# A two-layer hybrid decoder: sigmoid gates as hyperbolic tangents, and other places for weight blocks, token sums and small steps

## The chip, the cores and the metric

The kernel runs on one core of a Trainium2 chip. The metric is the device time of one execution in microseconds (us), lower is better. The engines are named as in the profile: PE multiplies matrices, PEld loads its stationary side, DVE (VectorE) and ACT (ScalarE) do elementwise work, POOL (GpSimd) does small elementwise work and issues accumulating DMAs, SP issues the other DMAs. Each engine works through its own instructions strictly in order.

## The reference

Two layers over 512 tokens of width 1024, all in float32:

```python
def hybrid_layer(x, ...):
    z = rmsnorm(x, norm_mix) @ w_in          # q_a k_a v_a | q_m k_m v_m o_m if_m | gates
    att = sliding_window_attention(...)      # 8 query heads, 2 key heads, window 128
    hm = rmsnorm(mlstm_chunkwise(...), m_head_norm)
    hm = hm * jax.nn.sigmoid(o_m)
    g_a, g_m = jnp.split(gates, 2, axis=-1)
    mixed = jax.nn.sigmoid(g_a) * (att @ w_att_branch) + jax.nn.sigmoid(g_m) * (hm @ w_m_branch)
    x = x + mixed @ w_out
    u = jax.nn.relu(rmsnorm(x, norm_ffn) @ w_ff1)
    return x + (u * u) @ w_ff2
```

So a layer has three sets of sigmoids: gate A (1024 x 512 values), gate M (as many) and the output gate `o_m` (512 x 512).

## The kernel before, in words

Every float32 matrix is split into a high part (`wh`, `ah`: ACT copies it to the matmul's rounded type) and a low part (`wl`, `al`: DVE subtracts the high part), and a product is three matmuls: high with high, high with low, low with high (`mm3`). So each weight block costs one DMA, one ACT copy and one DVE subtraction before PE can use it. `chunk` does this for the ordinary products: a raw tile `w` (pool `wraw`, 3 of them), then `wh` and `wl` (pool `wsp`, 4 of each), so the splits can run at most some blocks ahead of PE.

A layer has a mixer (function `mixer`) and an MLP. In the mixer, `weave` lays out the program: a row of filling matmul steps with a width of 0.25 each (a unit of 1.0 is one weight block of 12 wide matmuls), and side steps put in at chosen places on that scale. The recording layer then orders the instructions of each engine from it by priority and readiness, so a place is a wish and not an address. The filling row is: mLSTM queries and keys (8 blocks), gates 0 and 1 (gate A, `s0`, `s1`, 8 blocks each), product 2, the attention branch (`a_steps(0)`, `a_steps(1)`, 4 blocks each), products 5, 1, 3, 6, 7, 4 (4 short blocks of 6 wide matmuls each), gates 2 and 3 (gate M, `s2`, `s3`). Products 1 to 7 compute the mLSTM values and output gates with seven half-size products in place of eight: their weights are raw blocks `wa[k]` and `wb[k]` (k = 0 to 3) that are loaded by `begin` and `begin_other` and changed between products by accumulating DMAs on POOL's queue (`more`), and their tokens are sums of quarters of the normed input (`sums1`, `sums_next`, `sums3`, split by `sum_parts`).

The side steps are the attention's pieces (scores, softmax with Exp, transposed probabilities, output; places 7 to 24.2), the mLSTM gating (`gating0` to `gating3`: sums, a running maximum of four scans on DVE in `gating2`, its transposes on PE in `gating3`), the splits of queries and keys (`qk_split`), the mLSTM weights (`m_weights`: Exp) and outputs (`m_out`), and at the end the head norm `m_norm` (its `rsqrt` is Ln and then Exp on ACT) and the transposes of the heads (`head_tr`), which the last products need.

ACT holds one table set at a time. Exp and Ln are used from a set that has both (`LN_EXP`); Sigmoid is in another. The kernel before batches the sigmoids: `gates_a` runs the eight of gate A after the attention, `gates_o` the four output gates after product 4, `gates_m` the eight of gate M after the head norm's Exp, and `back` loads `LN_EXP` again.

Tiles of 128 x 512 come from two pools: `slot()` (pool `act`, 32 tiles) and `temp()` (pool `tmp`, 17 tiles). A tile is handed out again when its last user is done.

Of the kernel before, what the change touches and what calls it, by code (L numbers as in the profile page):

```python
# [33 lines left out]
def hybrid_kernel(ctx, tc, x, norm_mix, w_in, att_q_norm, att_k_norm, att_sinks, m_gate_bias,  # L34
# [199 lines left out]
    last_exp = [None]  # L234

    def rsqrt(dst, v, tag):

        shape = list(v.shape)
        t = sm(shape, tag + "t")
        sc.activation(t, v, AF.Ln)  # L240
        last_exp[0] = sc.activation(dst, t, AF.Exp, scale=-0.5)
# [148 lines left out]
    def mixer(l, norm, late, order, phase):  # L390
# [136 lines left out]
        for i, v_ in enumerate((v4[:, :NB - 1], dv4)):  # L527
            sc.activation(v2[:, i, :, :, 0, :], v_, AF.Copy)
            ve.tensor_tensor(v2[:, i, :, :, 1, :], v_, f32(v2[:, i, :, :, 0, :]), op=ALU.subtract)
# [16 lines left out]
        qT, sps, parts, att_last = {}, {}, {}, [None]  # L546
# [93 lines left out]
        def att_out(b, kv):  # L640
            po = aux()
            ls = parts[b, kv]
            for n, (pr, vb) in enumerate(ls):
                for m, p_ in enumerate(pr):
                    pe.matmul(po, vb.rearrange("p i d -> p (i d)"), p_, start=n + m == 0, stop=n == len(ls) - 1 and m == 1)
            low, both = temp(), temp()
            sc.activation(low[0:64, :], po[64:128, :], AF.Copy)
            p4, l4 = (t[0:64, :].rearrange("p (j i t) -> p j i t", j=2, i=2) for t in (po, low))
            b3 = both[:, 0:2 * P].rearrange("p (j t) -> p j t", j=2)
            for i in range(2):  # L650
                ve.tensor_tensor(b3[64 * i:64 * i + 64], p4[:, :, i, :], l4[:, :, i, :], op=ALU.add)
            for j in range(2):
                dh, dl = (a[:, b * P:(b + 1) * P] for a in att_acts[2 * kv + j])
                att_last[0] = sc.activation(dh, b3[:, j, :], AF.Copy)
                ve.tensor_tensor(dl, b3[:, j, :], f32(dh), op=ALU.subtract)
# [30 lines left out]
        def sigmoid(tiles):  # L686
            for t in tiles:
                i = sc.activation(t, t, AF.Sigmoid)
            return i

        def back(i):

            with tc.issue_after(i.ins):
                sc.preload_act_table_set(LN_EXP)  # L694

        def gate_steps(g, then=lambda: None):
            sg = []

            def ev(m, ps):
                sg.append(slot())  # L700
                ve.tensor_tensor(sg[m], ps, row[0], op=ALU.mult)  # L701
                if m == 3:
                    then()

            return sg, feat_steps(acts, wcols(C_G + 512 * g, 512), ev)
# [22 lines left out]
        def begin(k):  # L728
            wa[k] = temp()
            load(wa[k], 0, 0, k)  # L730
            gp.dma_start(wa[k], block(0, 1, k), accum_op=ALU.add)

        def begin_other(k):
            wb[k] = temp()
# [17 lines left out]
        def sum_parts(key, src):  # L752
            get = ((lambda: slot(F32R, (P, 2, H))) if key in (3, 6)
                   else lambda: now["tmp"].tile([P, 2, H], F32R, tag="t", name=nm("t")))
            sums[key] = [split(src[:, 2 * p:2 * p + 2, :], get=get) for p in range(2)]
# [44 lines left out]
        def gates_o():  # L800
            for b in range(NB):
                last = sc.activation(so[b], so[b], AF.Sigmoid, scale=norm.col[:, b:b + 1])
            back(last)
# [9 lines left out]
        def vo_step(n, k, i):  # L813
# [13 lines left out]
            if k == 3:  # L827
# [3 lines left out]
                if n == 4 and i == 1:  # L831
                    gates_o()
# [8 lines left out]
        for i, (b, kv) in enumerate(units):  # L841
# [6 lines left out]
            if kv == 0 and b + 1 < NB:  # L848
                if b + 2 < NB:
                    side += [(at + 1, lambda b=b: k_vec(b + 2)), (at + 1, lambda b=b: q_vec(b + 2))]  # L850
                side += [(at + 2 * 1.65 - 1.75, lambda b=b: k_tr(b + 1)), (at + 2 * 1.65 - 2.15, lambda b=b: q_tr(b + 1))]
        side += [(8.45, gating0), (25.5, gating1), (28.0, gating2), (30.5, gating3)]
        side += [(at, lambda m=m, i=i: qk_split(m, i))
                 for at, m, i in ((36.0, 0, 0), (36.6, 2, 0), (37.2, 0, 1), (37.8, 2, 1),
                                  (43.0, 1, 0), (43.8, 3, 0), (44.6, 1, 1), (45.4, 3, 1))]
        g0, s0 = gate_steps(0)
        def gates_a():
            with tc.issue_after(att_last[0].ins):
                back(sigmoid(g0 + g1))

        g1, s1 = gate_steps(1)
        side.append((7 + 1.65 * 7 + 3.45 + 2.2 + 0.01, gates_a))
# [30 lines left out]
        def m_out(h, t):  # L893
# [11 lines left out]
            if h:  # L905
                m_gate(h, t)

        def m_gate(h, t):
            c = slice(h * MV, (h + 1) * MV)
            ve.tensor_tensor(hm[t][:, c], hm[t][:, c], so[t][:, c], op=ALU.mult)  # L910
# [11 lines left out]
        def a_steps(g, sg):  # L922
            def ev_a(m, ps):
                t = sg[m]
                prod.append(t)
                ve.tensor_tensor(t, t, ps, op=ALU.mult)  # L926
# [4 lines left out]
        side += [(26.0 + 0.5 * k, lambda k=k: begin(k)) for k in range(4)]  # L931
        side += [(29.0 + 0.5 * k, lambda k=k: begin_other(k)) for k in range(4)]
# [516 lines left out]

    def turn_behind(norm, k):  # L1450

        with tc.issue_after(latest[0].ins):
# [4 lines left out]
            + [(6.5, lambda: gains(grow, 16))]  # L1457
# [53 lines left out]
```

## Time and profile before

| | |
|---|---|
| median of three runs | 1306.27 us (1303.46 to 1309.05) |
| the profiled execution | 1309.28 us, its span 1307.6 us |
| PE busy | 1287.5 us, 98% of the span, 6930 matmuls |
| DVE busy | 1012.1 us, 77% |
| ACT busy | 786.7 us, 60% |
| mean granted PE clock | 0.998 |
| places in the span | layer 0: mixer to about 345 us, MLP to about 650 us; layer 1: the same from there |

How to read it: the page's groups carry the line of the program, `out<-in` the names of tiles, `<-` the engine that ended an idle time. A row of the windows view gives, for a stretch from A to B, the busy time and instruction count of each engine, the granted PE clock, the busy share of the DMA engines and what they moved. A matmul's record is drawn longer (0.39 us for 512 columns) than the distance of two starts (0.23 us), so PE's records overlap.

### The profile page before, as it was taken

Reading aid. Unit: us, or ns where it says so; the run is one execution under the profiler, and the core shown is the slowest. Engines: PE = TensorE matmul, PEld = TensorE weight load, DVE = VectorE, ACT = ScalarE, POOL = GpSimd, SP = SyncE. Lnnn points to the kernel's source line nnn. Section 1 sums busy time; section 2 is a strip of 40 time slices with the busy share of each in tenths; the row PEclk is TensorE's granted clock in tenths of the full one; section 3 lists DMA queues with packets and bytes.
Section 4 is the critical chain, followed back from the end, with each engine's and each line's share of the span. In section 5 each row is a group of like instructions: output and inputs, shape, how many; then the busy total and the mean of one; then the engine's idle time right before and its main releaser. Section 6 shows DMA issues by size and latency. Waiting matters only on the chain. (4 is left out here: it accounts for less than half of the span.)

```text
span 1307.6 us, 19237 instructions
## 1 busy us (share of the span) xinstructions
PE 1287.5 (98%) x6930; PEld 1096.0 (84%) x6930; DVE 1012.1 (77%) x1605; ACT 786.7 (60%) x1375; POOL 224.2 (17%) x313
## 2 busy tenths in 40 slices
PE   9999999999999999999999999999999999999998
PEld 6877778888889999999888777788888899999987
DVE  4688888665677897978957888975737878879797
ACT  5567668543465665656554776884535556665563
POOL 4501141000003121131114011410000030311210
PEclk9999999999999999999999999999999999999999
DMA  5422672273358989898224227622714597988953
GB/s 154 110 74 57 154 147 68 68 241 98 97 145 162 230 191 203 204 203 233 33 69 115 64 62 190 117 73 76 254 58 127 137 206 207 203 208 201 208 147 97
DMA packets 135152, 186.01 MB, mean 142 GB/s; under 512 B 10376, under 2 KB 78832, under 8 KB 135056
## 3 DMA queue, kind: packets, MB, share of 16 engines
q1 hardware_dynamic: 94208, 131.82, 32.7%
q0 software_dynamic: 40128, 52.57, 25.6%
q8 instruction: 54, 0.88, 0.3%
q10 hardware_dynamic: 720, 0.40, 0.1%
q14 instruction: 42, 0.34, 0.1%
HBM read 182.65 MB, written 2.10 MB: 141 GB/s over the span
## 5 line engine op out<-in xcount | busy, mean ns | idle before, releaser
L47 PE MATMUL mm<-i,wh 128*128 128x512 f32 (+1 forms) x1280 | 353.9, 362 | 0.2
L1007 ACT ACTIVATE wh<-raw 128x1024 fp32r<-128x1024 f32 x212 | 223.3, 1056 | 188.1 <-PE mm L47 117.1
L1008 DVE TENSOR_TENSOR wl<-raw,wh 128x1024 fp32r<-128x1024 f32 x212 | 255.7, 1222 | 74.2 <-ACT wh L1007 74.2
L47 PEld LDWEIGHTS mm<-i,wh 128*128 128x128 f32 x1280 | 223.5, 189 | 31.3 <-DVE a L701 1.1
L47 PE MATMUL mm<-i,wl 128*128 128x512 f32 (+1 forms) x640 | 228.9, 359 | 0.0
L166 DVE TENSOR_TENSOR wl<-w,wh 128x512 fp32r<-128x512 f32 (+1 forms) x192 | 129.6, 679 | 101.9 <-ACT wh L165 97.4
L165 ACT ACTIVATE wh<-w 128x512 fp32r<-128x512 f32 (+1 forms) x192 | 116.6, 610 | 110.8 <-PE mm L47 77.5
L47 PE MATMUL mm<-wh,uh 128*128 128x512 f32 x440 | 171.8, 390 | 0.0
L47 PE MATMUL mm<-wl,uh 128*128 128x512 f32 x440 | 171.7, 390 | 0.0
L47 PE MATMUL mm<-wh,ul 128*128 128x512 f32 x440 | 171.2, 389 | 0.0
L1167 POOL DMA_DIRECT2D raw<-in_w_ff_dram x48 | 62.2, 1303 | 542.9 <-DMA raw<-in_w_ff_dram 143.9
L47 PEld LDWEIGHTS mm<-i,wl 128*128 128x128 f32 x640 | 121.0, 189 | 18.2 <-DVE wl L1008 0.6
L47 PE MATMUL mm<-wh,a 128*128 128x512 f32 x320 | 104.0, 398 | 0.7 <-ACT wh L724 0.7
L47 PE MATMUL mm<-wh,i 128*128 128x512 f32 (+1 forms) x352 | 101.4, 361 | 1.2 <-ACT wh L165 0.6
L1053 DVE SCALAR_TENSOR_TENSOR x<-mm,ms,x 128x512 f32<-128x512 f32 x126 | 90.8, 747 | 9.8 <-PE mm L47 9.8
L47 PEld LDWEIGHTS mm<-wh,ul 128*128 128x128 f32 x440 | 82.6, 188 | 17.4
L47 PEld LDWEIGHTS mm<-wh,uh 128*128 128x128 f32 x440 | 82.8, 188 | 16.1
L47 PEld LDWEIGHTS mm<-wl,uh 128*128 128x128 f32 x440 | 82.8, 188 | 15.6
L47 PE MATMUL mm<-a,wh 128*128 128x512 f32 x256 | 80.7, 395 | 2.3 <-DVE a L926 2.0
L47 PEld LDWEIGHTS mm<-wh,a 128*128 128x128 f32 x320 | 60.8, 190 | 14.6 <-ACT wh L724 1.5
L47 PEld LDWEIGHTS mm<-wh,i 128*128 128x128 f32 x352 | 61.9, 188 | 12.7 <-DVE i L179 1.8
L47 PE MATMUL aux<-i,wh 128*128 128x256 f32 x384 | 69.5, 283 | 0.0
(284 smaller groups left out, 2369.8 us busy)
## 6 DMA issues: line engine op xcount, KB each, us to landing
raw<-in_w_ff_dram SPq DMA_DIRECT2D x144, 512.0 KB, 5.1
raw<-in_w_ff_dram POOLq DMA_DIRECT2D x84, 512.0 KB, 7.9
w<-in_w_in_dram SPq DMA_DIRECT2D x112, 256.0 KB, 2.7
t<-in_w_in_dram POOLq DMA_DIRECT2D x32, 256.0 KB, 4.9
w<-in_w_out_dram SPq DMA_DIRECT2D x32, 256.0 KB, 3.2
w<-in_w_att_branch_dram SPq DMA_DIRECT2D x16, 256.0 KB, 3.0
t<-in_w_in_dram SPq DMA_DIRECT2D x16, 256.0 KB, 4.6
w<-in_w_m_branch_dram SPq DMA_DIRECT2D x16, 256.0 KB, 2.6
```

Of the source, the lines that this page charges most:

```text
L47: latest[0] = nc.tensor.matmul(*args, **kw)
L165: sc.activation(wh[:, :off], raw[:, :off], AF.Copy)
L166: ve.tensor_tensor(wl[:, :off], raw[:, :off], f32(wh[:, :off]), op=ALU.subtract)
L1007: sc.activation(hi, src, AF.Copy)
L1008: ve.tensor_tensor(lo, src, f32(hi), op=ALU.subtract)
L1053: ve.scalar_tensor_tensor(xh[:, cc], ps[i][:, cc], ms[j][:, b:b + 1], xh[:, cc], op0=ALU.mult, op1=ALU.add)
L1167: gp.dma_start(to[h], src(h, i, j), accum_op=ALU.add)
```

## The change

Since sigmoid(x) is half of 1 + tanh(x/2), the gates become Tanh on ACT with a scale of 0.5, the multiplications with them become (t + 1) times the other factor in one instruction (TENSOR_TENSOR becomes SCALAR_TENSOR_TENSOR), and the halves go into other factors: the attention's values (`v2`, scale 0.5) and the head norm's gain (0.25, in `late_gains`). The output gates have half the norm's column as their scale (`half`).

Each gate group now runs its four Tanh directly behind its evaluation (`ev`, at m = 3); only the last group loads `LN_EXP` again. Tanh is in a table set with Exp, not with Ln, so the program has four table loads in a layer (before the first Tanh, before the head norm's Ln, before its Exp, and at the end) where it had eight.

The raw blocks `wa`, `wb` are in `slot()` tiles and are begun at 24.5 and 28.0 instead of 26.0 and 29.0; all sums of tokens are in `temp()` tiles. `gating2` and `gating3` move from 28.0 and 30.5 to 30.5 and 35.5, the eight `qk_split` from 36.0 to 45.4 to the wider 37.0 to 48.0, `gates_o` from behind product 4 to 49.1, and the output gate's products of head 1 join those of head 0 at 49.3 and later.

```diff
-            sc.activation(v2[:, i, :, :, 0, :], v_, AF.Copy)
-            ve.tensor_tensor(v2[:, i, :, :, 1, :], v_, f32(v2[:, i, :, :, 0, :]), op=ALU.subtract)
+            sc.activation(v2[:, i, :, :, 0, :], v_, AF.Copy, scale=0.5)
+            ve.scalar_tensor_tensor(v2[:, i, :, :, 1, :], v_, 0.5, f32(v2[:, i, :, :, 0, :]), op0=ALU.mult,
+                                    op1=ALU.subtract)
...
-        def sigmoid(tiles):
-            for t in tiles:
-                i = sc.activation(t, t, AF.Sigmoid)
-            return i
-
-        def back(i):
-
-            with tc.issue_after(i.ins):
-                sc.preload_act_table_set(LN_EXP)
-
-        def gate_steps(g, then=lambda: None):
+        half = sm([P, NB], "half", 1)
+        ve.tensor_scalar(half, norm.col, 0.5, None, op0=ALU.mult)
+
+        def gate_steps(g, last=False):
             sg = []
             def ev(m, ps):
                 sg.append(slot())
                 ve.tensor_tensor(sg[m], ps, row[0], op=ALU.mult)
                 if m == 3:
-                    then()
+                    for t in sg:
+                        i = sc.activation(t, t, AF.Tanh, scale=0.5)
+                    if last:
+                        with tc.issue_after(i.ins):
+                            sc.preload_act_table_set(LN_EXP)
...
-            wa[k] = temp()
+            wa[k] = slot()
...
-            wb[k] = temp()
+            wb[k] = slot()
...
-            get = ((lambda: slot(F32R, (P, 2, H))) if key in (3, 6)
-                   else lambda: now["tmp"].tile([P, 2, H], F32R, tag="t", name=nm("t")))
-            sums[key] = [split(src[:, 2 * p:2 * p + 2, :], get=get) for p in range(2)]
+            sums[key] = [split(src[:, 2 * p:2 * p + 2, :],
+                               get=lambda: now["tmp"].tile([P, 2, H], F32R, tag="t", name=nm("t"))) for p in range(2)]
...
         def gates_o():
             for b in range(NB):
-                last = sc.activation(so[b], so[b], AF.Sigmoid, scale=norm.col[:, b:b + 1])
-            back(last)
+                sc.activation(so[b], so[b], AF.Tanh, scale=half[:, b:b + 1])
...
-                if n == 4 and i == 1:
-                    gates_o()
...
-        side += [(8.45, gating0), (25.5, gating1), (28.0, gating2), (30.5, gating3)]
+        side += [(8.45, gating0), (25.5, gating1), (30.5, gating2), (35.5, gating3)]
...
-                 for at, m, i in ((36.0, 0, 0), (36.6, 2, 0), (37.2, 0, 1), (37.8, 2, 1),
-                                  (43.0, 1, 0), (43.8, 3, 0), (44.6, 1, 1), (45.4, 3, 1))]
+                 for at, m, i in ((37.0, 0, 0), (38.0, 2, 0), (39.5, 0, 1), (41.0, 2, 1),
+                                  (43.5, 1, 0), (45.0, 3, 0), (46.5, 1, 1), (48.0, 3, 1))]
         g0, s0 = gate_steps(0)
-        def gates_a():
-            with tc.issue_after(att_last[0].ins):
-                back(sigmoid(g0 + g1))
-
         g1, s1 = gate_steps(1)
-        side.append((7 + 1.65 * 7 + 3.45 + 2.2 + 0.01, gates_a))
...
-            if h:
+            if h > 1:
                 m_gate(h, t)
...
-            ve.tensor_tensor(hm[t][:, c], hm[t][:, c], so[t][:, c], op=ALU.mult)
+            ve.scalar_tensor_tensor(hm[t][:, c], so[t][:, c], 1.0, hm[t][:, c], op0=ALU.add, op1=ALU.mult)
...
-                ve.tensor_tensor(t, t, ps, op=ALU.mult)
+                ve.scalar_tensor_tensor(t, t, 1.0, ps, op0=ALU.add, op1=ALU.mult)
...
-        side += [(26.0 + 0.5 * k, lambda k=k: begin(k)) for k in range(4)]
-        side += [(29.0 + 0.5 * k, lambda k=k: begin_other(k)) for k in range(4)]
+        side += [(24.5 + 0.5 * k, lambda k=k: begin(k)) for k in range(4)]
+        side += [(28.0 + 0.5 * k, lambda k=k: begin_other(k)) for k in range(4)]
...
-        side += [(46.8 + 0.2 * t, lambda t=t: m_gate(0, t)) for t in range(NB)]
+        side.append((49.1, gates_o))
+        side += [(49.3 + 0.9 * h + 0.15 * t, lambda h=h, t=t: m_gate(h, t)) for h in range(2) for t in range(NB)]
...
-        def gates_m():
-            with tc.issue_after(last_exp[0].ins):
-                back(sigmoid(g2 + g3))
-
-        g3, s3 = gate_steps(3, gates_m)
+        g3, s3 = gate_steps(3, True)
...
-                ve.tensor_tensor(sgm[g][m], sgm[g][m], ps, op=ALU.mult)
+                ve.scalar_tensor_tensor(sgm[g][m], sgm[g][m], 1.0, ps, op0=ALU.add, op1=ALU.mult)
...
+    def late_gains():
+
+        gains(grow, 16)
+        ve.tensor_scalar(gcol[:, 32:40], gcol[:, 32:40], 0.25, None, op0=ALU.mult)
```

Three places show how the instructions move. The first is ACT in layer 0 where gate A's values are turned into gates. In the rows of the kernel before, `a_632`, `a_634` are the attention's last output, `a_1342` to `a_1691` gate A's eight tiles, `wh` the high parts of weights, L796 the evacuation of product 2:

```order
L654 ACTIVATE a_634<-t_1710 128x128
L688 ACT_TABLE_LOAD
L688 ACTIVATE a_1342<-a_1342 128x512
L165 ACTIVATE wh_1836<-w_1834 128x512
L796 ACTIVATE t_1783<-mm_1693 128x512
L796 ACTIVATE t_1788<-mm_1694 128x512
L165 ACTIVATE wh_1871<-w_1869 128x512
L165 ACTIVATE wh_1891<-w_1889 128x512
L688 ACTIVATE a_1344<-a_1344 128x512
L688 ACTIVATE a_1346<-a_1346 128x512
L688 ACTIVATE a_1348<-a_1348 128x512
L688 ACTIVATE a_1685<-a_1685 128x512
```

In the changed kernel the first four stand in the middle of the attention; L582 writes a block's queries, L560 and L561 its keys:

```order
L165 ACTIVATE wh_1515<-w_1513 128x512
L582 ACTIVATE t_1248<-aux_1243,gc_137 64x2x128
L561 ACTIVATE kT_620<-aux_1291,gc_147 64x128
L698 ACT_TABLE_LOAD
L698 ACTIVATE a_1345<-a_1345 128x512
L698 ACTIVATE a_1347<-a_1347 128x512
L698 ACTIVATE a_1349<-a_1349 128x512
L165 ACTIVATE wh_1568<-w_1566 128x512
L698 ACTIVATE a_1351<-a_1351 128x512
L582 ACTIVATE t_1253<-aux_1243,gc_137 64x2x128
L560 ACTIVATE kT_620<-aux_1291,gc_147 64x128
L561 ACTIVATE kT_620<-aux_1291,gc_147 64x128
```

So half of gate A's work on ACT, with the only load of its set, is now ahead of the second half of the attention, and nothing of it is left behind the attention. The other four Tanh stand some 40 rows further down, between the last blocks' outputs.

The second place is ACT at products 3, 6 and 7. L724 (L722 in the changed kernel) are the high parts of the raw blocks, L789 (L786) the evacuation of product 3, L872 (L861) the decay rows of the mLSTM weights. Before:

```order
L802 ACT_TABLE_LOAD
L802 ACTIVATE t_1783<-t_1783,ncol_374 128x512
L724 ACTIVATE wh_2216<-t_1807 128x512
L724 ACTIVATE wh_2230<-t_1818 128x512
L789 ACTIVATE vm_2069<-mm_2026,minus_2071 128x4x128
L724 ACTIVATE wh_2238<-t_1846 128x512
L789 ACTIVATE vm_2069<-mm_2027,minus_2071 128x4x128
L872 ACTIVATE t_2202<-aux_2200 128x512
L802 ACTIVATE t_1788<-t_1788,ncol_374 128x512
L724 ACTIVATE wh_2265<-t_1887 128x512
L724 ACTIVATE wh_2282<-t_1901 128x512
L880 ACT_TABLE_LOAD
```

In the changed kernel:

```order
L722 ACTIVATE wh_2190<-a_1893 128x512
L799 ACTIVATE t_1794<-t_1794,half_637 128x512
L799 ACTIVATE t_1799<-t_1799,half_637 128x512
L722 ACTIVATE wh_2207<-a_1732 128x512
L722 ACTIVATE wh_2215<-a_1747 128x512
L722 ACTIVATE wh_2232<-a_1782 128x512
L786 ACTIVATE vm_2071<-mm_2019,minus_2073 128x4x128
L861 ACTIVATE t_2201<-aux_2199 128x512
L786 ACTIVATE vm_2071<-mm_2020,minus_2073 128x4x128
L722 ACTIVATE wh_2240<-a_1801 128x512
```

Both table loads are gone from between the high parts, and the first two output gates stand a step earlier, ahead of the first block of product 6 (`wh_2207`; before, `wh_2208`, two rows ahead of the first load shown).

The third place is PE at the transposes of the running maximum (`t_1855` before, `t_1919` in the changed kernel, written by DVE's four scans). Before, they are strewn singly into the second attention-branch product:

```order
L47 MATMUL mm_1944<-a_629,wh_1918 128x512
L52 MATMUL aux_1931<-ident,t_1855 128x4
L47 MATMUL mm_1944<-a_628,wl_1919 128x512
L47 MATMUL mm_1915<-a_630,wh_1960 128x512
L47 MATMUL mm_1915<-a_631,wh_1960 128x512
```

In the changed kernel all four stand behind the third block of product 5:

```order
L47 MATMUL mm_2020<-wh_2043,t_1835 128x512
L47 MATMUL mm_2020<-wl_2044,t_1835 128x512
L47 MATMUL mm_2020<-wh_2043,t_1836 128x512
L52 MATMUL aux_2056<-ident,t_1919 128x4 x4
L47 MATMUL mm_2019<-wh_2063,t_1835 128x512
```

The first transpose stood in the first block of `a_steps(1)` (its weights are `wh_1918`); now three more blocks of that product and three short blocks of product 5 lie ahead of it.

More of the change, by code (lines that the diff above doesn't have):

```diff
@@ L232, in weave @@
             f()
-    last_exp = [None]
     def rsqrt(dst, v, tag):
@@ L240, in rsqrt @@
         sc.activation(t, v, AF.Ln)
-        last_exp[0] = sc.activation(dst, t, AF.Exp, scale=-0.5)
+        sc.activation(dst, t, AF.Exp, scale=-0.5)
         t2 = sm(shape, tag + "u")
@@ L545, in mixer @@
         att_acts = [(slot(F32R), slot(F32R)) for _ in range(4)]
-        qT, sps, parts, att_last = {}, {}, {}, [None]
+        qT, sps, parts = {}, {}, {}
         tri_i = tri_l.bitcast(I32)
@@ L653, in att_out @@
                 dh, dl = (a[:, b * P:(b + 1) * P] for a in att_acts[2 * kv + j])
-                att_last[0] = sc.activation(dh, b3[:, j, :], AF.Copy)
+                sc.activation(dh, b3[:, j, :], AF.Copy)
                 ve.tensor_tensor(dl, b3[:, j, :], f32(dh), op=ALU.subtract)
@@ L1456, in hybrid_kernel @@
             + [(3.0, lambda: load_late(4)), (4.0, lambda: load_late(6))]
-            + [(6.5, lambda: gains(grow, 16))]
+            + [(6.5, late_gains)]
             + [(3.0 + 2.2 * j, lambda j=j: norm.squares(j)) for j in range(2)])
```

## The prediction

> **What bounds the kernel now.** I read the page first, then the windows of PE over both layers, then PE's rows where a window has idle time, and ACT and DVE just ahead of those places. The page's first part says that PE is the bound:
>
> ```profile
> PE 1287.5 (98%) x6930; PEld 1096.0 (84%) x6930; DVE 1012.1 (77%) x1605; ACT 786.7 (60%) x1375; POOL 224.2 (17%) x313
> ```
>
> The change takes no wide matmul away and adds none, so it can only gain what PE stands still, and only where it does. The windows show where. First ten microseconds of an MLP (columns: PE, PEld, DVE, ACT, POOL busy and counts, PE clock, DMA share, GB/s):
>
> ```profile
> 290.00:300.00 10.00, 10.00 (x46) 8.06 (x45) 9.12 (x16) 4.97 (x9) 0.00 (x0) 1.00 0.61 202
> ```
>
> Then stretches of layer 0's mixer, and below them of layer 1's:
>
> ```profile
> 70.00:104.00 34.00, 32.45 (x168) 25.73 (x166) 28.72 (x71) 25.77 (x79) 1.28 (x2) 1.00 0.24 66
> 104.00:141.00 37.00, 36.09 (x174) 28.50 (x174) 33.50 (x82) 25.28 (x80) 6.74 (x11) 1.00 0.23 64
> 156.30:169.50 13.20, 10.40 (x42) 7.17 (x42) 12.30 (x23) 5.55 (x11) 2.58 (x3) 1.00 0.92 216
> 169.50:203.00 33.50, 31.39 (x129) 24.74 (x129) 27.91 (x44) 25.17 (x45) 12.95 (x18) 0.95 0.66 112
> 203.00:222.00 19.00, 18.61 (x95) 14.93 (x93) 15.80 (x44) 18.19 (x45) 3.30 (x9) 1.00 0.25 71
> ```
>
> ```profile
> 805.60:818.50 12.90, 11.56 (x48) 8.18 (x48) 11.96 (x24) 4.19 (x8) 2.58 (x3) 1.00 0.92 203
> 818.50:850.00 31.50, 30.28 (x135) 24.62 (x134) 28.93 (x50) 27.37 (x51) 13.82 (x21) 1.00 0.70 118
> 850.00:868.00 18.00, 17.61 (x89) 14.04 (x87) 14.63 (x42) 16.95 (x41) 2.42 (x6) 1.00 0.31 87
> ```
>
> Outside the mixers PE stands still for nothing, and in the mixers for some microseconds at a few places: the attention (70 to 141: 1.55 + 0.91 us), the second attention-branch product (2.80 and 1.34 us in the two layers), products 5 to 7 (2.11 and 1.22 us, in layer 0 with a granted clock of 0.95 besides), and the stretch with the second pair of output gates (0.39 us each). These rows understate the loss, since a matmul's record is longer than the distance of two starts. Here are PE's rows at the first three losses of layer 0:
>
> ```profile
> 155.59 0.61 PE L47 MATMUL mm<-a,wh 128*128 128x512 f32 x2
> 156.05 0.39 PE L47 MATMUL mm<-a,wl 128*128 128x512 f32 x1
> 158.15 0.73 PE L47 MATMUL mm<-a,wh 128*128 128x512 f32 x2 [1.72 <-DVE a L926]
> ...
> 161.62 0.19 PE L52 MATMUL aux<-ident,t 4*128 4x4 f32 x1 [0.94 <-DVE t L476]
> ...
> 190.16 0.50 PE L47 MATMUL mm<-wh,a 128*128 128x512 f32 x1 [0.66 <-ACT wh L724]
> 191.88 0.50 PE L47 MATMUL mm<-wl,a 128*128 128x512 f32 x1 [1.22 <-DVE wl L725]
> 192.92 1.05 PE L47 MATMUL mm<-wh,a 128*128 128x512 f32 x2
> ```
>
> Two starts lie 0.23 us apart (155.59 to 156.05 for two). So 42 matmuls in the 13.20 us window fill 9.7 us of it and 3.5 are lost, not 2.80; in 805.60:818.50, 48 fill 11.0 and 1.9 are lost; in 169.50:203.00, 129 fill 29.7 and 3.8 are lost, with the matmuls from 192.92 that ran at half pace after the two waits (1.05 us for two). For 818.50:850.00 the count gives 0.4 (narrow matmuls are among them), so its idle 1.22 stands. With 0.39 twice for the stretches behind, the pool is 3.5 + 1.9 + 3.8 + 1.2 + 0.8 = 11.2 us; the attention's idle time of 2.5 us a layer is beside it.
>
> **What the change removes.** The late gate A. ACT's and DVE's rows ahead of the loss at 156:
>
> ```profile
> 141.01 1.28 ACT L688 ACT_TABLE_LOAD   x1
> 146.04 2.70 ACT L688 ACTIVATE a<-a 128x512 f32<-128x512 f32 x5
> 153.00 0.63 ACT L165 ACTIVATE wh<-w 128x512 fp32r<-128x512 f32 x1 [3.21 <-DMA w<-in_w_att_branch_dram]
> 154.18 1.28 ACT L694 ACT_TABLE_LOAD   x1
> 155.47 1.15 ACT L175 ACTIVATE t<-sc 128x512 fp32r<-128x512 f32 x2
> 156.21 1.29 DVE L176 TENSOR_TENSOR t<-sc,t 128x512 fp32r<-128x512 f32 x2 [0.71 <-ACT t L175]
> 157.42 1.28 DVE L926 TENSOR_TENSOR a<-a,mm 128x512 f32<-128x512 f32 x2
> ```
>
> Five sigmoids of 0.54 us and a load of 1.28 delay the high parts of the branch's weights, so their raw tiles come free late, the next DMA starts late, and a second load stands ahead of the token sums (L175). DVE waits there for ACT with L176, and L926, which frees PE's banks, is queued behind it: PE waits 1.72 us. All of this ACT work is gone from here, so L926 should start when PE is done. The wait of 0.94 us for the scan (L476) goes by another edit: its transposes now stand six blocks later. DVE needs three evacuations, a low part, a fourth evacuation and a scan for them after the product's end, some 3.8 us at 0.6 to 0.7 each, of which 2 run ahead of the end; PE has three short blocks, 3 x 6 x 0.23 = 4.1 us. I leave 0.5 of 3.5 and 0.5 of 1.9: **4.4 us gained**.
>
> The output gates and the query and key splits. Ahead of the waits of 0.66 and 1.22 us:
>
> ```profile
> 186.36 1.10 DVE L680 TENSOR_TENSOR a<-a,a 64x512 fp32r<-64x512 f32 x1
> 187.57 1.28 ACT L802 ACT_TABLE_LOAD   x1
> 188.79 1.01 DVE L680 TENSOR_TENSOR a<-a,a 64x512 fp32r<-64x512 f32 x1
> 191.15 1.88 DVE L725 TENSOR_TENSOR wl<-t,wh 128x512 fp32r<-128x512 f32 x3
> 195.52 1.28 ACT L880 ACT_TABLE_LOAD   x1
> ```
>
> The four subtractions of `qk_split`'s first half (L680 and, between them, L683) stand on DVE ahead of three low parts, and ACT has a load and a gate ahead of their high parts. The changed order has no load here (2 x 1.28 less on ACT), and two of the four subtractions are up in product 5, the others with a low part between. Two short blocks of product 6 take PE 2.7 us, with two low parts and two subtractions on DVE 2.5. With the waits the half pace goes, too. I leave 0.8 of 3.8 and 0.4 of 1.2: **3.8 us**. The second pair of output gates loses its two loads: 0.2 of 0.8 left, **0.6 us**. The early raw blocks and sums in small tiles only make these steps ready sooner; none is waited for by PE in the rows above, so I count nothing for them, and if their loads crowd the weights' DMAs (share 0.92 in the window), it is in the 0.5 left. Sum of gains 8.8 us.
>
> **What it adds.** Four Tanh and a load in the attention, ahead of a weight's high part and the next block's queries. I price a Tanh as a sigmoid, 0.54, so the block is 1.28 + 4 x 0.54 = 3.4 us, gate 1's is 2.2. Just there ACT stands idle, and gate A's values come from DVE meanwhile:
>
> ```profile
> 107.22 0.63 ACT L165 ACTIVATE wh<-w 128x512 fp32r<-128x512 f32 x1 [2.79 <-issue]
> ```
>
> ```profile
> 103.58 1.28 DVE L701 TENSOR_TENSOR a<-mm,t 128x512 f32<-128x512 f32 x2
> 105.37 1.28 DVE L701 TENSOR_TENSOR a<-mm,t 128x512 f32<-128x512 f32 x2
> ```
>
> The idle time runs from 104.4 to 107.2: the load fits into 104.4 to 105.7, three Tanh reach to 107.3, where the high part could start anyway; one Tanh, 0.5 us, is left over. Bounds: nothing, and 3.4 + 2.2 = 5.6 us a layer if all of it reached PE. I take 0.4 a layer (near the lower end, because the idle 2.79 covers most), 0.8 in all. The multiplications become SCALAR_TENSOR_TENSOR; the nearest row of that form against the one replaced:
>
> ```profile
> L791 DVE SCALAR_TENSOR_TENSOR vm<-mm,minus,vm 128x512 f32<-128x512 f32 x8 | 6.0, 748 | 2.5 <-PE mm L47 2.5
> L926 DVE TENSOR_TENSOR a<-a,mm 128x512 f32<-128x512 f32 x16 | 10.6, 682 | 0.5 <-PE mm L47 0.5
> ```
>
> 0.07 us more for 32 of them, on PE's path only where a bank is waited for: 0.4 (bounds 0 and 2.2). At the mixer's end two loads now stand in the head norm's chain:
>
> ```profile
> 255.83 0.22 ACT L240 ACTIVATE hqt<-hss 128x16 f32<-128x16 f32 x1 [0.51 <-DVE hss L913]
> 260.45 0.69 DVE L918 TENSOR_TENSOR a<-a,hr 128x512 f32<-128x512 f32 x1
> 263.26 0.60 PE L52 MATMUL aux<-ident,a 128*128 128x128 f32 x4
> ```
>
> 2 x 1.28 = 2.57 us, 0.51 of the first in ACT's wait; PE asks for the result 263.26 - 261.14 = 2.1 us after it is there. So nothing, just; the bound is 2.57 - 2.1 = 0.5 a layer. The Trainium skill, ScalarE: Activation LUTs (Table sets: the hidden batching unit), speaks against this edit: batch by table set, since Ln and Exp share one and need one load. Its section What ACT_TABLE_LOAD costs adds about 1.38 us of emptying to each load's 1.28; by that the chain would be 5.3 us and PE would wait 3.2 a layer (an estimate from that page), 6.4 us in all. The trace does not agree on the emptying: the load at 154.18 ends at 155.46, and L175 starts at 155.47.
>
> Sum: 8.8 - 1.2 = 7.6 us less than the profiled 1309.28, 1301.7. That execution was 3.0 above the median, so against the median **1298.7 us**; by the same shift below. Unknowns give 1294 (all of the 11.2 us, plus some of the attention's) to 1304 (6 us gained, 4 spent).
>
> **The rivals.**
> - *DVE takes over.* In the window 156.30:169.50 DVE is busy 12.30 of 13.20 us, in 818.50:850.00 28.93 of 31.50. If DVE rather than ACT sets these stretches, half of the gain stays: 4.4 - 1.2, so 1303. Against it: DVE's waits for ACT (0.71 at 156.21).
> - *The attention pays (slower).* ACT's Tanh blocks hold up scores and softmax, DVE (33.50 of 37 busy) has no room to catch up, and every later attention step on PE, in order, comes late. 5.6 us a layer is 11.2; the token sums and splits, which follow the attention, come late too, which halves the gain to 4.4, and two waits as long as that at 191 bring the half pace, 1.7 us each: + 11.2 + 3.4 - 4.4 = + 10, so 1316 to 1317. It decides where the block passes 2.79 us by more than the attention's own slack.
> - *The head norm decides.* If the loads also wait for the engine to be empty, both layers pay at the transposes: by rows 0.5 to 1.1 us a layer (the high part between Ln and Exp, 0.6, waits as well), so 1300. The skill page named above is the reason to keep it.
> - *The attention gains.* Keys' copies come earlier than before (L560, L561 stand ahead of the scores); if its idle time halves, 2.5 us more, 1295.
>
> That the change does not do what it says is excluded by the order: four loads a layer.
>
> **How the numbers follow.** A measurement of this kernel can tell about 0.5% from no change, 6.5 us, so faster is below 1299.7, slower above 1312.8. My forecast has a chance of 0.58, DVE takes over 0.14, the attention pays 0.18, the head norm 0.04, the attention gains 0.06. Of the forecast's own range about 0.65 lies below 1299.7 (0.38), of DVE's 0.2, of the head norm's half, and all of the last: 0.49, say 0.50. Slower is the attention's case, 0.18. The rest, 0.32, is the same. The forecast's own range is 1294 to 1304; for 8 in 10 the range goes to 1290 and into the slow case, to 1314.
>
> **What would show it.** Right: no PE wait over 0.5 us between the attention's end and product 5, a clock of 1.00 all through layer 0, no row of L724's successor (L722) waited for, four loads a layer, ACT's idle time at the first Tanh gone. Wrong: new PE waits of over 0.5 us between 104 and 141 on scores or probabilities; PE waiting for the transposes at the mixer's end; DVE's low parts (L723) still ending waits in products 5 to 7.

## The result and the profile after

The changed kernel takes 1299.42 us (median of 6 runs, 1298.39 to 1300.42) against 1307.41 us before (6 runs, 1303.46 to 1309.72): a ratio of 0.994, with a 95% interval of 0.992 to 0.996. The profiled execution took 1299.13 us with a span of 1297.4.

The first part of the page, busy time by engine:

```profile
PE 1282.7 (99%) x6930; PEld 1095.2 (84%) x6930; DVE 1008.3 (78%) x1608; ACT 776.3 (60%) x1367; POOL 236.2 (18%) x313
```

ACT has 10.4 us less, eight table loads of 1.28 us each. The windows of layer 0 that the prediction showed (columns as there), and, 8 us earlier than before, those of layer 1:

```profile
104.00:141.00 37.00, 36.56 (x176) 28.93 (x176) 32.97 (x80) 30.79 (x87) 7.95 (x12) 1.00 0.28 80
156.30:169.50 13.20, 12.59 (x56) 10.00 (x57) 13.14 (x24) 5.88 (x10) 9.61 (x7) 1.00 0.27 54
169.50:203.00 33.50, 33.03 (x153) 26.65 (x151) 30.33 (x57) 26.80 (x56) 12.11 (x19) 1.00 0.68 120
203.00:222.00 19.00, 18.98 (x102) 16.02 (x102) 15.70 (x53) 15.58 (x49) 2.88 (x9) 1.00 0.37 98
...
797.60:810.50 12.90, 11.62 (x52) 9.20 (x52) 12.84 (x23) 6.12 (x11) 8.45 (x5) 1.00 0.21 45
810.50:842.00 31.50, 30.52 (x135) 24.12 (x135) 27.63 (x50) 22.96 (x48) 11.75 (x18) 1.00 0.74 134
```

Layer 0's windows gained, and the clock is 1.00 in them. Layer 1's second attention-branch product (797.6 to 810.5) hardly did: PE has 1.28 us of idle time there, against 1.34 before, with 52 matmuls in it against 48. The waits of PE by what ended them:

```profile
PE mm L47 <- DVE a L915: 3.2, 4, 1.4
PE mm L47 <- DVE wl L723: 1.0, 2, 0.5
```

And PE's rows at the longest of them, one in each layer:

```profile
155.20 0.39 PE L47 MATMUL mm<-a,wl 128*128 128x512 f32 x1
156.50 0.73 PE L47 MATMUL mm<-a,wh 128*128 128x512 f32 x2 [0.91 <-DVE a L915]
...
796.88 0.39 PE L47 MATMUL mm<-a,wl 128*128 128x512 f32 x1
798.67 0.73 PE L47 MATMUL mm<-a,wh 128*128 128x512 f32 x2 [1.40 <-DVE a L915]
```

This is the wait that the prediction wanted gone, at the same bank evacuation (L926 before, L915 now). ACT's and DVE's rows ahead of it show that its cause is another:

```profile
147.81 0.63 ACT L165 ACTIVATE wh<-w 128x512 fp32r<-128x512 f32 x1 [1.45 <-DMA w<-in_w_att_branch_dram]
150.12 0.64 ACT L165 ACTIVATE wh<-w 128x512 fp32r<-128x512 f32 x1 [1.68 <-DMA w<-in_w_att_branch_dram]
...
154.49 1.31 ACT L165 ACTIVATE wh<-w 128x512 fp32r<-128x512 f32 x2 [2.58 <-DMA w<-in_w_att_branch_dram]
```

```profile
155.16 0.69 DVE L166 TENSOR_TENSOR wl<-w,wh 128x512 fp32r<-128x512 f32 x1 [1.02 <-ACT wh L165]
155.77 2.47 DVE L915 SCALAR_TENSOR_TENSOR a<-a,mm 128x512 f32<-128x512 f32 x4
```

ACT no longer stands behind sigmoids, but waits for the branch's weights to land. DVE waits for ACT's high part with L166, and the four evacuations are queued behind that instruction, as before the change.

To put a number on each stretch, the distance of every matmul to the next start is compared with the usual one for its width (0.227 us for 512 columns), and what is over is summed (pieces of up to some 0.02 us left out). Layer 0's stretches are given in us; layer 1's lie 650 us later before and 642 later after (640 in the kernel of the last column). The last two columns are the experiments below in which only the activations changed, and in which all but the raw blocks and sums changed.

| stretch | before, layers 0 + 1 | after | activations alone | old raw blocks |
|---|---|---|---|---|
| 70 to 104 | 3.9 + 4.0 | 4.1 + 4.1 | 4.1 + 4.2 | 4.1 + 4.1 |
| 104 to 141, attention | 2.6 + 2.5 | 2.2 + 2.1 | 2.2 + 2.1 | 2.2 + 2.1 |
| 141 to 172, branch products | 4.6 + 3.2 | 2.2 + 2.7 | 1.2 + 1.2 | 0.5 + 0.5 |
| 172 to 203, products 5 to 7 | 4.7 + 1.9 | 1.2 + 1.8 | 1.7 + 1.9 | 0.6 + 0.4 |
| 203 to 232, output gates | 2.3 + 2.3 | 1.2 + 1.3 | 1.4 + 1.3 | 1.2 + 1.2 |
| 232 to 280, head norm | 1.3 + 1.1 | 1.0 + 1.0 | 1.0 + 1.0 | 1.0 + 0.9 |
| sum | 34.4 | 24.9 | 23.3 | 18.8 |

From before to after that is 9.5 us, of the 10.15 us between the two profiled executions.

### The profile page after: what moved, and what is told of

Its sections match the earlier page's. It is cut to its first block, busy times and chain, and to the rows that moved or that the text cites. A ratio compares the mean times of both kernels' runs of the same rounds, so it can differ in the third digit from the quotient of the medians.

```text
span 1297.4 us, 19218 instructions
## 1 busy us (share of the span) xinstructions
PE 1282.7 (99%) x6930; PEld 1095.2 (84%) x6930; DVE 1008.3 (78%) x1608; ACT 776.3 (60%) x1367; POOL 236.2 (18%) x313
## 4 chain that ended last, share of the span: by engine, by line
PE 91%; DVE 3%; DMA 3%; ACT 2%; issue 1%; DVEq 0%; SPq 0%; ACTq 0%
PE mm L47 73%; PE aux L47 16%; PE aux L52 2%; DMA w<-in_w_in_dram 2%; DMA w<-in_w_att_branch_dram 1%; ACT wh L165 1%; DVE wl L166 1%; ACT t L615 0%; DVE wl L723 0%; DVE t L583 0%; DVE a L915 0%; DMA x<-in_x_dram 0%; DVE t L620 0%; DVE m L609 0%; DVE t L176 0%
## 5 line engine op out<-in xcount | busy, mean ns | idle before, releaser
L166 DVE TENSOR_TENSOR wl<-w,wh 128x512 fp32r<-128x512 f32 (+1 forms) x192 | 129.0, 675 | 100.7 <-ACT wh L165 96.3
L1152 POOL DMA_DIRECT2D raw<-in_w_ff_dram x48 | 62.2, 1303 | 543.0 <-DVE i L179 234.2
L47 PEld LDWEIGHTS mm<-wh,ul 128*128 128x128 f32 x440 | 82.6, 188 | 17.5
L47 PE MATMUL mm<-wh,a 128*128 128x512 f32 x256 | 81.4, 393 | 0.0
L1309 POOL DMA_DIRECT2D raw<-in_w_ff_dram x36 | 43.6, 1212 | 149.2 <-DVE wl L993 103.3
L47 PE MATMUL aux<-t,wh 128*128 128x256 f32 x384 | 69.5, 283 | 0.0
```

Of the source, the lines that this page charges most:

```text
L47: latest[0] = nc.tensor.matmul(*args, **kw)
L166: ve.tensor_tensor(wl[:, :off], raw[:, :off], f32(wh[:, :off]), op=ALU.subtract)
L1152: gp.dma_start(to[h], src(h, i, j), accum_op=ALU.add)
L1309: gp.dma_start(to[h], src(h, i, j), accum_op=ALU.add)
```

## The experiments

**The two halves of the change.** The activations alone: `gates_o` behind product 4, raw blocks, sums, scans and splits as before.

> The changed activations alone (four table loads a layer instead of eight, tanh in place of the batched sigmoids, the halved values and gains); raw blocks, sums, scans, query and key splits and the place of the output gates as in the kernel before. Theory, that the loads and batches on ScalarE delayed the high parts and through DVE's order the bank evacuations: the wait on L926's successor at 156 us shrinks, but the wait for the scan's transposes (0.94 us) and part of the waits at 190 us stay; some 4 us less than before, ratio about 0.997. Rival, that the moves alone make the gain: ratio 1.000. Rival, that the shorter ScalarE work is all that counts: ratio 0.994, as the full change.

Measured: 1297.33 us (1297.10 to 1297.82), ratio 0.992 (0.991 to 0.994). The moves alone, on the kernel before:

> The moves alone (raw blocks in early tiles, sums in small tiles, scans later, query and key splits spread), with the batched sigmoids and eight table loads a layer as before. Theory: the wait for the scan's transposes goes (about 1 us a layer) and some of the waits of products 5 to 7, but the wait for gate A's batch stays, and the early raw loads now stand ahead of the branch's weights: 1 to 3 us less than before, ratio 0.998 to 0.999. Rival, that the moves alone make the gain: ratio 0.994.

Measured: 1306.59 us, ratio 0.9995 (0.998 to 1.001). So the theory put too little on the activations. They bring 10 us, 2 more than the whole change; the moves bring nothing to the median by themselves and take 2 us away beside the activations. In the kernel with the moves alone the stretch at gate A's batch is even worse than before:

```profile
150.00:172.00 22.00, 18.14 (x76) 14.40 (x74) 17.70 (x29) 11.22 (x19) 6.33 (x6) 0.92 0.48 110
```

PE loses 3.86 us of 22 and some of its clock. But products 5 to 7 of layer 0 have no idle time in the same trace and a full clock, where the kernel before lost 2.11 us between 169.5 and 203 at a clock of 0.95, though both table loads and the gates still stand between their high parts on ACT (at 184.5 and 190.9 us):

```profile
172.00:203.00 31.00, 31.00 (x143) 25.47 (x142) 28.14 (x52) 26.58 (x53) 10.85 (x16) 1.00 0.69 121
```

So in layer 0 the moves lose at one place and win at another.

**The raw blocks put back.** From the changed kernel:

```diff
-            wa[k] = slot()
+            wa[k] = temp()
-            wb[k] = slot()
+            wb[k] = temp()
...
-        side += [(24.5 + 0.5 * k, lambda k=k: begin(k)) for k in range(4)]
-        side += [(28.0 + 0.5 * k, lambda k=k: begin_other(k)) for k in range(4)]
+        side += [(26.0 + 0.5 * k, lambda k=k: begin(k)) for k in range(4)]
+        side += [(29.0 + 0.5 * k, lambda k=k: begin_other(k)) for k in range(4)]
```

and the sums of keys 3 and 6 in `slot` again.

> The changed kernel with only the raw blocks and the sums put back to their old tiles and times. My prediction counted nothing for their move: equal to the changed kernel, 0.994 of before. Theory from the trace, that the early raw loads crowd the branch's weights and so make the two stalls that are left (1.08 us at 155 and 1.56 us at 797): these stalls shrink, and the kernel is 1 to 3 us faster than the changed one unless products 5 to 7 now wait for raw blocks. Rival, that the old place delays the raw blocks: 1 to 3 us slower than the changed kernel, with waits for DMA at product 5.

Measured: 1293.40 us (1292.68 to 1294.29), ratio 0.989 (0.988 to 0.991): 6 us faster than the changed kernel, twice what the theory gave it, and 3.9 us faster than the activations alone, so the other moves do gain beside them. No wait is left in products 1 to 7 of either layer. The windows (141 to 203 us, and 791 to 822 of layer 1) have no idle time at all on PE:

```profile
141.00:172.00 31.00, 31.00 (x150) 25.37 (x149) 30.17 (x62) 14.03 (x26) 7.51 (x9) 1.00 0.88 210
172.00:203.00 31.00, 31.00 (x141) 25.24 (x140) 28.68 (x57) 27.69 (x61) 13.02 (x21) 1.00 0.56 105
...
791.00:822.00 31.00, 31.00 (x142) 25.32 (x141) 30.63 (x50) 19.14 (x34) 10.48 (x14) 1.00 0.85 179
```

DVE is busy for 30.17 of 31 us there and holds nobody up. The landing times of the branch's weights, from the DMA part of the page (last column: median us from issue to landing), of the changed kernel and of this one:

```profile
w<-in_w_att_branch_dram SPq DMA_DIRECT2D x16, 256.0 KB, 5.4
```

```profile
w<-in_w_att_branch_dram SPq DMA_DIRECT2D x16, 256.0 KB, 3.5
```

The last two of layer 0, issued between 146 and 150 us, took 7.3 and 5.9 us to land in the changed kernel and 4.0 and 3.3 in this one.

**Is it their time or their tiles?** The changed kernel with only the two numbers 24.5 and 28.0 put back to 26.0 and 29.0:

> The changed kernel with the raw blocks begun at the old places of the side plan (26.0 and 29.0) but in the changed kernel's own tiles, and with the sums as changed. It tells the time of the loads from the kind of tile. If the crowding of the branch's weights by time is all: with free tiles the loads still start at once, some 3 us later than in the changed kernel, so part of the stalls at 155 and 797 us stays; between the changed kernel (0.994) and the one with old raw blocks (0.989), about 0.992. If the old tiles, which came free one by one and so spread the loads, made the difference: the stalls stay, 0.994 or worse. If only the start counts: 0.989.

Measured: 1299.68 us (1299.13 to 1300.13), ratio 0.994: nothing is won back, and the second theory of the expectation holds. With tiles that are free from the start the loads do not keep to the plan's numbers; SP issues them between 135 and 150 us in this kernel and in the changed one. SP's queue, in the changed kernel and in the one with old raw blocks:

```profile
135.62 0.43 SPq L713 DMA_DIRECT2D a<-in_w_in_dram  x1
137.98 0.33 SPq L155 DMA_DIRECT2D w<-in_w_att_branch_dram  x1
138.36 1.38 SPq L713 DMA_DIRECT2D a<-in_w_in_dram  x3
141.40 2.26 SPq L155 DMA_DIRECT2D w<-in_w_att_branch_dram  x3
```

```profile
135.17 7.07 SPq L155 DMA_DIRECT2D w<-in_w_att_branch_dram  x4
142.33 0.38 SPq L713 DMA_DIRECT2D t<-in_w_in_dram  x1
```

In `temp` tiles, which come free later, the loads stand further down in SP's order, and nine of the sixteen have a wait put ahead of them (none in the changed kernel). So five branch weights were issued ahead of the first raw block (four of them in the rows shown), where the changed kernel had two. The old tiles were a brake: in the changed kernel twelve transfers of 256 KB (eight loads and four accumulations) run among the branch's weights, and the brake kept half of them out. The sums' tiles went back with the blocks in the kernel before this one, and with neither here; they were not tried apart. The kernels below keep the sums in their changed tiles and reach the same time, so the gain does not need the old ones.

**Time alone, the other way.** The changed kernel with tiles as changed, and the loads begun at `17.0 + 0.8 * k` and `20.6 + 0.8 * k`, in the attention:

> The changed kernel with the raw blocks' loads moved up into the attention, begun at 17.0 and 20.6 of the side plan, 0.8 apart, where the DMA share is 0.23 (tiles as in the changed kernel). Theory, that these loads crowd the branch's weights: landing times of the branch weights fall from 5.4 us to about 3, the stalls at 155 and 797 us go, 2 to 3 us faster than the changed kernel, ratio about 0.992. Rival, that DVE's own work sets this stretch: the stalls stay and the time is that of the changed kernel, 0.994. Rival, that the loads disturb the attention's weights: slower by 1 us or more, with waits for weights between 115 and 135 us.

Measured: 1293.84 us (1292.21 to 1295.70), ratio 0.990 (0.988 to 0.992): 5.6 us faster than the changed kernel, twice what the theory gave. The branch's weights land in 2.9 us (median) and the stalls at 155 and 797 are gone, and with them those on L723. With old raw blocks, which are loaded later, these are gone as well, so they were a consequence of the crowding. So it is the traffic and not the tiles that costs. The third case of the expectation came in part: PE has a new wait in the attention, not for weights but for POOL's selections (here the one of layer 0; POOL's rows below it).

```profile
117.65 1.17 PE L47 MATMUL aux<-t,v 128*128 128x512 f32 x4 [1.42 <-DVE t L650]
```

```profile
114.09 0.86 POOL L729 DMA_DIRECT2D a<-in_w_in_dram  x1 [2.05 <-DMA a<-in_w_in_dram]
114.65 2.59 POOL L635 TENSOR_SCALAR_AFFINE_SELECT t<-t 128x512 fp32r<-128x512 f32 x3
```

The accumulating DMA waits on POOL for its block's load, and the attention's selections are queued behind it. Two kernels test that. In the first the four accumulations stand behind the last selection:

> The kernel with the raw loads in the attention (ratio 0.990 of before), with the accumulating DMAs of the first blocks, which wait on GpSimd's queue for these loads, moved behind the attention's last selections. Theory, that those waiting DMAs held up the attention's selections (L635) and so PE's waits of 1.6 and 2.3 us at 116 and 756: these waits go, 3 us less, ratio 0.987 to 0.988, the fastest of all. Rival, that the loads themselves are in the attention's way: the waits stay, 0.990.

Measured: 1298.50 us (1298.07 to 1299.81), ratio 0.993. The waits in the attention went, as the theory had it, but the time did not: four accumulations issued from 133.7 us on crowd the branch's weights as eight loads had done. The weight issued at 137.3 us took 7.1 us to land, against 2.5 with old raw blocks. ACT's row:

```profile
144.52 0.63 ACT L165 ACTIVATE wh<-w 128x512 fp32r<-128x512 f32 x1 [4.06 <-DMA w<-in_w_att_branch_dram]
```

In the second they stand two and two behind the selections of the third and the second unit from the end:

> The kernel with the raw loads in the attention, with the accumulating DMAs two and two behind the selections of the third and the second unit from the attention's end: late enough that GpSimd waits for no load, and ahead of the branch's weights. If the two causes found are all (GpSimd's queue held by the waiting DMAs, worth 1.4 and 2.3 us of PE's time; the branch's weights crowded by raw blocks), neither the waits at 116 and 756 nor those at 145 and 155 are there: 3 us less than with the accumulations first, about 1290.5 us, ratio 0.987. If any raw traffic in the attention costs PE time: 0.990 as with the accumulations first, or worse.

Measured: 1292.43 us (1291.84 to 1293.28), ratio 0.989 (0.987 to 0.991). Neither wait is there, so both causes are shown; the size was 2 us off (the trace that it was worked out from was of the slowest run of its kernel, 1295.70). This kernel and the one with old raw blocks, at the same ratio, are the fastest tried.

**The scans and the splits.** Both from the kernel with old raw blocks (1293.40). First the second and third gate sums back from 30.5 and 35.5 to 28.0 and 30.5:

> The changed kernel with old raw blocks and sums (ratio 0.989 of before), and the second and third step of the gate sums put back to 28.0 and 30.5. Theory, that DVE's scan stands behind the bank evacuations of the attention-branch products: PE waits for the scan's transposes again, 0.5 to 1 us a layer, 1 to 2 us slower, ratio 0.990 to 0.991. Rival, that the scan only waited because gate A's batch delayed everything before it: no wait, 0.989.

Measured: 1295.03 us (1294.75 to 1295.05): 1.6 us slower, as the theory had it, but not in its way. No wait for the scan's transposes (0.94 us before) is in the trace, as the rival said. The loss by starts grows by 0.7 us a layer in the branch products, in small pieces, and these stand at the four transposes of the running maximum. Here they come singly between wide matmuls, as in the kernel before; in the base they come in a row (PE's rows of this kernel, then of the base):

```profile
156.83 0.39 PE L47 MATMUL mm<-a,wh 128*128 128x512 f32 x1
157.15 0.22 PE L52 MATMUL aux<-ident,t 4*128 4x4 f32 x1
157.30 0.50 PE L47 MATMUL mm<-a,wl 128*128 128x512 f32 x1
157.64 0.62 PE L47 MATMUL mm<-a,wh 128*128 128x512 f32 x2
...
169.87 0.39 PE L47 MATMUL mm<-wh,t 128*128 128x512 f32 x1
170.19 0.41 PE L52 MATMUL aux<-ident,t 4*128 4x4 f32 x4
170.53 0.50 PE L47 MATMUL mm<-wh,t 128*128 128x512 f32 x1
170.86 0.40 PE L47 MATMUL mm<-wl,t 128*128 128x512 f32 x1
```

Two wide matmuls alone take 2 x 0.227 us. With one transpose between them it is 0.81 us (156.83 to 157.64), so 0.36 more; with four it is 0.99 (169.87 to 170.86), so 0.54 more. Four single ones cost 1.4 us a layer and four in a row 0.54, which makes 1.8 us in both layers, near the 1.6 measured. Then the splits of queries and keys back at their old places:

> The changed kernel with old raw blocks and sums (ratio 0.989 of before), and the splits of queries and keys put back to their old places. Theory, that four subtractions of 1.0 to 1.1 us in a row ahead of product 6's low parts make PE wait: 0.5 to 1.5 us in layer 0 and less in layer 1, 1 to 3 us slower in all, ratio 0.990 to 0.992. Rival, that the table loads alone made those waits: 0.989.

Measured: 1294.08 us (1294.01 to 1295.25), 0.7 us slower with ranges that overlap, less than the theory gave. The long waits of products 5 to 7 (0.66 and 1.22 us before) do not come back, so the old places of the splits do not make them without the loads and ACT's gate. Nor did the loads and the gate make them without the old places, in layer 0 of the kernel with the moves alone. So either half of the change takes these waits away; which of the moves does it was not tried apart.

**Loads in the head norm.** The same base, with two more loads between Ln and Exp:

```diff
-        sc.activation(t, v, AF.Ln)
+        i = sc.activation(t, v, AF.Ln)
+        if tag == "hq":
+            with tc.issue_after(i.ins):
+                sc.preload_act_table_set("gelu_and_others")
+                sc.preload_act_table_set("sigmoid_and_others")
```

> The changed kernel with old raw blocks and sums, and two more table loads in the head norm's chain of each layer, between its Ln and its Exp: four there in place of two. By the trace a load holds ScalarE for 1.28 us, and the next instruction starts 0.01 us behind it; PE has next to no slack left at the transposes, so PE waits 2.0 to 2.6 us a layer more: 4 to 5 us slower than with two loads, ratio 0.993. If each load also empties the engine for about another microsecond: 5 us a layer, 10 us in all, ratio 0.997. If the head norm had slack to spare: 0.989.

Measured: 1293.63 us (1293.07 to 1293.87): the same as without. The first two cases of the expectation are out. ACT's rows:

```profile
248.68 1.28 ACT L242 ACT_TABLE_LOAD   x1
249.97 1.28 ACT L243 ACT_TABLE_LOAD   x1
251.27 0.22 ACT L243 ACTIVATE hr<-hqt 128x16 f32<-128x16 f32 x1
```

Each load holds ACT for 1.28 us and the next instruction starts 0.01 to 0.02 us behind it. The third case held by its number, but the base had no slack of that size: its last normed block is ready at 253.09 us, and the four transposes that read the blocks start from 253.01 us on. In this kernel's order PE asks for the transposes block by block and not four at once, and waits 0.26 us; by starts the stretch loses 0.7 us more a layer.

**Loads in the attention.** The same base, with two more loads around gate 0's tanh:

```diff
                     for t in sg:
                         i = sc.activation(t, t, AF.Tanh, scale=0.5)
+                        if g == 0 and t is sg[0]:
+                            with tc.issue_after(i.ins):
+                                sc.preload_act_table_set("gelu_and_others")
```

> The changed kernel with old raw blocks and sums (ratio 0.989 of before), and two more table loads in the attention of each layer: one behind gate 0's first tanh, one ahead of the next softmax's Exp, 2.57 us of ScalarE in all. If the attention pays for what ScalarE does there (the slower rival of the prediction), all of it reaches PE: 2.6 us a layer, 5 us in all or more, ratio 0.993. If the idle time in the attention covers it, as the prediction held for most of the first load: 0 to 2 us, ratio 0.989 to 0.991.

Measured: 1310.91 us (1307.47 to 1311.81), ratio 1.003 (1.001 to 1.004): 17.5 us slower than the base, more than three times the worst case. PE's rows at the attention's end and the window behind them:

```profile
140.06 0.39 PE L47 MATMUL mm<-wh,i 128*128 128x512 f32 x1
143.98 1.09 PE L52 MATMUL aux<-ident,t 128*128 128x128 f32 x4 [3.53 <-DVE t L620]
...
141.00:152.00 11.00, 7.41 (x28) 5.93 (x29) 6.47 (x18) 5.71 (x19) 3.90 (x5) 0.58 0.74 182
```

The last unit's probabilities (L620) are computed at 143.15 us, and the branch product, which needs that unit, has nothing left to put ahead of it. PE stands for 3.5 us, and its granted clock is 0.50 from 144 to 156 us. In the base L620 runs at 130.69 us, 12.5 us earlier, which 2.57 us of loads do not explain by themselves. The order of PE's instructions is another one here, since the recording layer's scheduler counts the loads, so this is the price of the loads with what the scheduler makes of them, and not that of ACT's time alone.

## Why the prediction was right, and where its sum was not

The time (1299.42 against 1298.7) and its direction were right. That the sum came so near is luck: terms were mis-sized in both directions, and the shift in the last point hid what did not cancel.

- *Gate A's stall and the scan* (4.4 us forecast). After: 2.9 us by the table (7.8 to 4.9). The mechanism was right: without the batch and its load the high parts come in time, and with old raw blocks 6.8 of the 7.8 us go. The scan's wait went with the batch, too, and not by its own move: with the activations alone and the scans at their old place it is not there. What that move gains, 1.6 us, is a term that the sum did not have: transposes in a row instead of singly. The step that failed is the sentence that the early raw blocks cost nothing beyond "the 0.5 left". Putting them back gains 6.0 us, 3.9 in this stretch and 2.0 in the next. The row to see it in was quoted, a DMA share of 0.92; I took the loads for work that only becomes ready sooner and did not ask what had held them back.
- *Output gates and splits* (3.8). 3.6 us after, nearly all in layer 0 with the half pace; 5.6 without the raw blocks. Right in size, but the crowding takes back in layer 1 what the edits gave, and in layer 0 the moves alone do as much (0.4 us left by starts).
- *Second pair of output gates* (0.6). 2.1 us by starts: the idle time of 0.39 a layer that I took for the pool shows about a third of the 1.0 to 1.1 us that went.
- *Tanh in the attention* (0.4 a layer lost). It gained 0.4 a layer. The block stood as worked out, and nothing slid:

```profile
104.38 1.28 ACT L698 ACT_TABLE_LOAD   x1
105.67 1.68 ACT L698 ACTIVATE a<-a 128x512 f32<-128x512 f32 x3
107.25 0.61 ACT L165 ACTIVATE wh<-w 128x512 fp32r<-128x512 f32 x1
```

- *The other form of multiplication* (0.4). Nothing: one takes no longer than the TENSOR_TENSOR that it replaced (682 ns).

```profile
L915 DVE SCALAR_TENSOR_TENSOR a<-a,mm 128x512 f32<-128x512 f32 x16 | 10.0, 678 | 0.0
```

- *Head norm* (0). Right, and just: in the changed kernel the last of the four normed blocks is ready at 255.51 us, and PE starts their transposes at 255.44, with no wait in the list. For the experiment with loads in the head norm, the Trainium skill, ScalarE: Activation LUTs (What ACT_TABLE_LOAD costs), would make the chain's four loads 10.6 us (an estimate from that page, 2.66 us each); the trace does not agree, since no load there is followed by an empty stretch.
- *The shift of 3.0 us* from the profiled run to the median did not carry over: the changed kernel's profiled run is 0.3 us under its median. In profiled times the forecast was 1301.7 and the result 1299.13, so 2.6 us of gain were missed, and the shift hid it.

Of the rivals, "DVE takes over" is out: with DVE 30.17 of 31 us busy PE stands still for nothing. "The attention pays" did not come. With 2.57 us more on ACT there and the order that the scheduler then chose, it did, at 8.7 us a layer where the rival had 5.6; what of it is ACT's time stays open. "The head norm decides" is out, since PE waits for no transpose there. "The attention gains" came in small: 0.8 us between 104 and 141 by the table, with 0.3 lost ahead of it. Of the signs, the clock of 1.00, the four loads and the filled idle time were as said; "no PE wait over 0.5 us" failed at 155 us (0.91) and in layer 1 at 797 (1.40), and of the wrong signs the waits for L723 appeared.

## What to carry to other kernels

A tile that comes free late also holds its load back; before giving a load a tile that is free at once, list what else is in flight on the same queue and engines at that moment, and whose landing PE waits for first. A DMA issued on POOL that had to wait for another DMA (2.05 us here) held up the selections behind it, so look at what stands behind such a DMA on its engine. Small transposes are better put in a row than strewn among wide matmuls (0.54 us for four against 1.4). And price an edit's parts apart: here one half gained 10 us, and the other, harmless by itself, cost 2 beside it: 6 lost in one of its pieces and 4 gained in the rest.

## What the runs showed of the hardware

- With the extra loads in the attention the granted clock was 0.58 in the 11 us from 141 on, which hold most of a PE wait of 3.5 us, and still 0.89 in the 20 us behind them. Between 144 and 156 us it was 0.50, with PE busy for 11.39 of these 12 us.

```profile
152.00:172.00 20.00, 20.00 (x82) 16.09 (x81) 17.21 (x36) 6.19 (x11) 2.04 (x3) 0.89 0.50 132
```

- The kernels whose trace holds such a stretch spread widely from run to run: 8.9 us for the kernel before (17 runs, 1302.72 to 1311.61), 5.3 for the moves alone (12 runs), 4.3 with loads in the attention (12 runs); without such a stretch the changed kernel spreads 2.0, the activations alone 0.7, the loads in the attention's time 3.5 (6 runs each). The longer runs are those with the lower mean clock: of the 17 of the kernel before, the three at 1.000 took 1303.75 us on average and the four at 0.996 and 0.997 took 1309.6; with the moves alone, the two at 0.999 took 1304.4 and the six at 0.996 took 1307.7. Whether the clock or the waits ahead of it make the spread was not tested.
- Four 256 KB accumulations issued within 3.6 us were enough to stretch the landing of one branch weight from 2.5 to 7.1 us, and ACT stood 4.06 us for it.
- A small transpose (4*128 4x4 in its row) cost PE 0.36 us between two wide matmuls, and four in a row 0.54 us together.
